# The first mixing of a two-block network: x scaled by its norm factor ahead of the transposes, raw x transposed a second time

## The chip, the core and the metric

The kernel runs on one core of a Trainium2 chip. The metric is device time in microseconds (us) of one execution; three runs of the kernel before gave 2796.80, 2799.38 and 2799.76 us, median 2799.38 us. TensorE multiplies matrices, VectorE and ScalarE work on elements, GpSimd does a few element operations beside them, and SyncE issues most transfers. In the profile they are PE (with PEld for its weight loads), DVE, ACT, POOL and SP.

## The reference, cut to what matters

Two blocks in float32 over 512 tokens of 1024 features. The change lies in the first block's mixing:

```python
h = rms_norm(x, attn_norm_w[i])          # x * rsqrt(mean(x*x) + eps) * w
g_q, g_k, g_v, g_z, g_b, g_a, s_u, d_q, d_k, d_v = split_cols(h @ w_in[i], IN_SIZES)
qkv = silu(causal_dwconv(concat([g_q, g_k, g_v]), gdn_conv_w[i]))   # 4 taps along the tokens
o_gdn = gated_delta_chunked(l2norm(g_q), l2norm(g_k), g_v, beta, log_decay)
o_gdn = rms_norm(o_gdn, gdn_norm_w[i]) * silu(g_z)
o_s5 = rms_norm(s5_mixer(s_u, ...), s5_norm_w[i])
o_diff = diff_attention(d_q, d_k, d_v, lam)
x = x + concat([o_gdn, o_s5, o_diff]) @ w_out[i]
x = x + conv_glu_ffn(rms_norm(x, ffn_norm_w[i]), ...)
```

Then come two layers of feed-forward, second mixing and feed-forward, and a last norm. The factor rsqrt(mean + eps), one number per token, can be applied to x before the product or to the columns of the product after it; both give the same result.

## The kernel before

Activations lie with features on the 128 partitions and the 512 tokens along the free axis, eight tiles for 1024 features. Every product of two float32 operands is made of three matmuls: each operand is split into a high part (rounded) and a low part (the rest), and `product` (L329 on) sums low weight times high x, high weight times low x and high times high. One product of 128 outputs is thus 8 times 3 = 24 matmuls of 512 columns, into one of the two PSUM buffers of tag `pp`. Each weight unit is loaded (`wr`), rounded on ScalarE (`wh`) and its rest taken on VectorE (`wl`); `wh` and `wl` have two buffers.

`first_load` brings x in as four blocks of 128 tokens, token on the partition. TensorE transposes them into all eight PSUM banks, and from the banks ScalarE makes the high parts `xgh` (times the gain) and VectorE the low parts `xgl`, in halves of 256 tokens; both engines then copy the raw x to `xT`. Square sums on ScalarE, an inverse square root in 10 small VectorE operations (`rsqrt`) and a spread over the partitions through TensorE (`spread`, tile `rT`) give `self.r`, the norm factor in every partition. So the first products start without the norm factor, and every reader of one multiplies by it afterwards on VectorE: `su` (four), `ab` (one), `dq`, `dk`, `dv` (four each), `gpad` (twelve, the convolution's padded input) and the gate `zs` in tile `gcv` (four).

`weave` (L346 on) writes the work of parts that run side by side in one order, by due times that each part yields; a scheduler then sets the final order of each engine, which is fixed before the run. The first mixing has two stages. In the first, the s5 tables are computed on VectorE, then four rounds of s5 (`WB`, `w4j`, `KT`, `ca`, `can`, `rho`, `z`), the gates and four heads of differential attention run side by side, with the 17 products as filler for TensorE. In the second, the four heads of the gated delta rule (`gdn`) do the same with their 16 products and those of the output weights. GpSimd makes `W` and `w4t` of s5, three operations for each round.

Of the kernel before, what the change touches and what calls it, by code (L numbers as in the profile page):

```python
# [244 lines left out]
class Net:  # L245
# [461 lines left out]
    def first_load(self, sp):  # L707

        nc, gain = self.nc, self.col["attn_norm"]
        self.sel = self.const.tile([128, 4, 128], F32, name="sel")  # L710
        nc.gpsimd.memset(self.sel, 0.0)
        nc.gpsimd.dma_start(out=self.sel[0:8], in_=self.A["sel"])
        one = self.tmp.tile([128, 128], F32, name="one", tag="sq")
        nc.gpsimd.memset(one, 1.0)
        self.ones = self.const.tile([128, 128], F32R, name="ones")
        nc.gpsimd.tensor_copy(out=self.ones, in_=one)

        zero = self.tmp.tile([128, 128], F32, name="zero", tag="sq")
        nc.gpsimd.memset(zero, 0.0)
        self.hl = self.const.tile([128, 128], F32R, name="hl")  # L720
        nc.gpsimd.tensor_copy(out=self.hl, in_=zero)
        blocks = []
        for n in range(4):
            src = self.A["x"][n * 128:n * 128 + 128]
            if n < 2:
                t = [self.op.tile([128, S], F32R, name=f"x{c}", tag=f"g{c}").bitcast(F32) for c in "hl"]
                for i in range(2):
                    nc.sync.dma_start(out=t[i], in_=src[:, i * S:i * S + S])
            else:
                w = self.wraw.tile([128, D], F32, name="wr", tag="wr")  # L730
                nc.sync.dma_start(out=w, in_=src)
                t = [w[:, :S], w[:, S:]]
            blocks.append(t)
        ps = [self.pp.tile([128, S], F32, name="pp", tag="pp") for _ in range(2)]
        ps += [f() for f in (self.ps, self.ps, self.ps, self.po, self.po, self.po)]
        v2, v = self.c4("v2", (128, 4, 2)), self.c4("cv")
        self.xs = [tuple(self.xgp.tile([128, S], F32R, name=f"xg{c}{k}", tag=f"xg{c}{k}") for c in "hl")
                   for k in range(KD)]
        at = lambda half, k, n=0, w=256: ps[4 * half + k // 2][:, 256 * (k % 2) + 128 * n:][:, :w]
        cs = [slice(256 * half, 256 * half + 256) for half in range(2)]  # L740
        for half, c in enumerate(cs):
            for n in range(2):
                for k in range(KD):
                    b = blocks[2 * half + n][k // 4]
                    nc.tensor.transpose(at(half, k, n, 128), b[:, (k % 4) * 128:(k % 4) * 128 + 128], self.ident)
            for k in range(KD):
                (h, l), g = self.xs[k], gain[:, k:k + 1]
                self.act(h[:, c], at(half, k), AF.Copy, scale=g)
                self.stt(l[:, c], at(half, k), g, h[:, c].bitcast(F32), ALU.mult, ALU.subtract)
        self.ready[12] = self.weights(self.A["w_in"][12], KD)  # L750
        for half, c in enumerate(cs):
            for k in range(KD):
                if k % 2:
                    nc.scalar.copy(out=self.xT[k][:, c], in_=at(half, k))
                else:
                    nc.vector.tensor_copy(out=self.xT[k][:, c], in_=at(half, k))
        for n in range(4):
            for i in range(2):
                sq = self.tmp.tile([128, S], F32, name="acc", tag="acc")
                self.act(sq, blocks[n][i], AF.Square, accum_out=v2[:, n, i:i + 1])  # L760
        self.tt(v, v2[:, :, 0], v2[:, :, 1], ALU.add)
        self.ts(v, v, 1.0 / D, ALU.mult, EPS, ALU.add)
        p = self.ps()
        self.at_once(self.spread(p, self.rsqrt(v)))
        self.r = self.bc.tile([128, S], F32, name="rstd", tag="rstd")
        nc.scalar.copy(out=self.r, in_=p)

    def out_after(self, outs, keys, w, pace=0):

# [8 lines left out]
        self.added.add(w)  # L778

    def proj(self, unit):  # L780
        return self.product(self.A["w_in"][unit], self.xs, self.ready.pop(unit, None))

    def scaled(self, pool, p, tag, bufs=None):
        t = pool.tile([128, S], F32, name=tag, tag=tag, bufs=bufs)
# [15 lines left out]
    def diff(self, dp, small, lane, nlam, outs):  # L800
        nc = self.nc
        gain = small.tile([128, 1], F32, name="dgain", tag=f"dgain{lane}", bufs=1)
        self.ts(gain, self.col["diff_norm"], 1.0 - LAM_INIT, ALU.mult)
        for h in (lane, lane + 2):
            slot = lambda name, k: self.x_slot(name, 4 * lane + k)
            ts = []
            for c, name in enumerate(("dq", "dk", "dv")):
                ts.append(slot(name, c))
                self.tt(ts[-1], self.proj(3 * h + c), self.r, ALU.mult)
                yield 5.2, (0, 0, 1.0)[c]  # L810
            qT, kT, vT = ts
            pv = self.transposed([vT[:, n * 128:n * 128 + 128] for n in range(4)])
            vt = slot("dvt", 3).rearrange("p (n v) -> p n v", n=4)
            nc.scalar.copy(out=vt, in_=pv.rearrange("p (n v) -> p n v", n=4))
            yield 0.25, 0
            po = self.po()
            eps = small.tile([128, 4], F32, name="eps", tag="eps", bufs=2)
            for qb in range(4):
                n = (qb + 1) * 128
                es = []  # L820
                for c in range(2):
                    rows = slice(64 * c, 64 * c + 64)
                    p = self.ps()
# [130 lines left out]
    def s5(self, sp, sq, tables, outs):  # L954
        nc = self.nc
        M = ALU.mult
        K, th8, pre, pim, B1, B2, C1, C2 = tables
        uts, ys = [], []
        for i in range(4):
            uts.append(self.scaled(sp, self.proj(12 + i), f"su{i}"))  # L960
            yield 5.2, 0
        pool = nc.gpsimd
        for i in range(4):
# [57 lines left out]
            self.reduced(sq, ca, [128, 512], "ca")  # L1021
            sn, cs = self.sincos(sq, ca, [128, 512], "ca")
            rho = sq.tile([128, 512], F32, name="rho", tag="rho")
            nc.vector.tensor_copy(out=v8(rho), in_=th8[:, 1, G].unsqueeze(2).to_broadcast(shc))
            nc.vector.memset(v8(rho)[:, :, 0:1], 0.0)
            yield 0.5, 1.0

# [63 lines left out]
    def gates(self, gc):  # L1091
# [1 line left out]
        M = ALU.mult  # L1093
        p = self.proj(16)
        ab = self.tmp.tile([8, S], F32, name="ab", tag="sq")
        self.tt(ab, p[0:8], self.r[0:8], M)
        yield 5.2, 1.0
        pt = self.ps()
        for n in range(4):
# [45 lines left out]
    def gdn(self, gf, gp, K, h, locks, outs):  # L1145
# [9 lines left out]
        for c in range(3):  # L1155
            p = self.proj(17 + 4 * h + c)
            i = 4 * c + h
            taps = self.col["gdn_conv"][:, 4 * i:4 * i + 4]
            pad = gf.tile([128, S + 3], F32, name="gpad", tag="gpad")
            nc.gpsimd.memset(pad[:, 0:3], 0.0)  # L1160
            self.tt(pad[:, 3:], p, self.r, M)
            cv = gf.tile([128, S], F32, name="gcv", tag="gcv")
            self.act(cv, pad[:, 3:], AF.Copy, scale=taps[:, 3:4])
            for t in (2, 1, 0):
                self.stt(cv, pad[:, t:t + S], taps[:, t:t + 1], cv, M, ALU.add)
            o = gf.tile([128, S], F32, name=f"g{c}", tag=f"g{c}")
            self.act(o, cv, AF.Silu)
            qkv.append(o)
            yield 5.2, 0
# [142 lines left out]
        self.stages += 1  # L1312
        third.n += 1
        yield from self.take(parked)
        zs = self.scaled(gf, self.proj(17 + 4 * h + 3), "gcv")
        self.act(zs, zs, AF.Silu)
        yield 5.2, 0
        self.stt(ss, ss, 1.0 / 128, vq, M, ALU.add)
        rr = self.rsqrt(ss)
# [211 lines left out]
```

## Time and profile before

| | |
|---|---|
| median of three runs | 2799.38 us |
| the profiled execution | 2799.44 us, span 2797.7 us |
| PE busy | 2723.6 us, 97% of the span |
| DVE busy | 1602.2 us, 57% |
| ACT busy | 1047.8 us, 37% |
| POOL busy | 167.4 us, 6% |
| chain that ended last | PE 87%, DVE 8%, ACT 2%, issue 2% |

A matmul of 512 columns stands in the records with 0.39 us, while the next one starts 0.23 us after it, so PE's busy time is no measure of how full it is where short gaps occur: the sum overlaps the gaps. The chain of waits shows better which engine the end depends on. The first mixing takes about 510 of the 2798 us; the rest of the program has the same instructions in both kernels.

### The profile page before, as it was taken

Reading aid. Unit: us, or ns where it says so; the run is one execution under the profiler, and the core shown is the slowest. Engines: PE = TensorE matmul, PEld = TensorE weight load, DVE = VectorE, ACT = ScalarE, POOL = GpSimd, SP = SyncE. Lnnn points to the kernel's source line nnn. Section 1 sums busy time; section 2 is a strip of 40 time slices with the busy share of each in tenths; the row PEclk is TensorE's granted clock in tenths of the full one; section 3 lists DMA queues with packets and bytes.
Section 4 is the critical chain, followed back from the end, with each engine's and each line's share of the span. In section 5 each row is a group of like instructions: output and inputs, shape, how many; then the busy total and the mean of one; then the engine's idle time right before and its main releaser. Section 6 shows DMA issues by size and latency. Waiting matters only on the chain.

```text
span 2797.7 us, 33414 instructions
## 1 busy us (share of the span) xinstructions
PE 2723.6 (97%) x12880; PEld 2188.6 (78%) x12880; DVE 1602.2 (57%) x2949; ACT 1047.8 (37%) x1712; POOL 167.4 (6%) x188
## 2 busy tenths in 40 slices
PE   8989999999999999999999999999999999999997
PEld 6667887788887888876778888888888766788886
DVE  8887865874666433447675434444344666643443
ACT  4556533442344322333453223333233345432223
POOL 1100000100001000012010000000000300100001
PEclk9999999999999999999999999999999999999999
DMA  5003110323323233231122232332333311323322
GB/s 185 27 20 106 61 39 27 110 96 90 101 88 101 98 89 108 84 119 57 34 78 96 89 102 98 90 103 92 100 98 89 102 38 45 100 98 89 107 84 82
DMA packets 83521, 239.13 MB, mean 85 GB/s; under 512 B 9304, under 2 KB 20952, under 8 KB 83232
## 3 DMA queue, kind: packets, MB, share of 16 engines
q1 hardware_dynamic: 82368, 233.53, 26.7%
q8 instruction: 101, 1.65, 0.2%
q0 software_dynamic: 416, 2.03, 0.2%
q10 hardware_dynamic: 576, 1.42, 0.1%
q14 instruction: 60, 0.49, 0.1%
HBM read 232.75 MB, written 4.19 MB: 85 GB/s over the span
## 4 chain that ended last, share of the span: by engine, by line
PE 87%; DVE 8%; ACT 2%; issue 2%; POOL 0%; DMA 0%; ACTq 0%; DVEq 0%; POOLq 0%
PE pp L288 75%; PE ps L288 6%; PE ps L481 2%; PE po L288 2%; DVE wl L291 2%; ACT wh L301 1%; ACT xgh L301 0%; DVE cr L298 0%; DVE ct L298 0%; DVE pd L291 0%; DVE xT L291 0%; DVE ct L291 0%; ACT sq L301 0%; DVE z L291 0%; POOL acc L291 0%
## 5 line engine op out<-in xcount | busy, mean ns | idle before, releaser
L301 ACT ACTIVATE wh<-wr 128x1024 fp32r<-128x1024 f32 (+6 forms) x543 | 476.8, 879 | 1288.4 <-PE pp L288 873.5
L288 PE MATMUL pp<-xgh,wl 128*128 128x512 f32 x2264 | 894.6, 395 | 16.7 <-DVE wl L291 8.0
L288 PE MATMUL pp<-xgh,wh 128*128 128x512 f32 x2264 | 887.8, 392 | 0.0
L288 PE MATMUL pp<-xgl,wh 128*128 128x512 f32 x2264 | 886.9, 392 | 0.0
L291 DVE TENSOR_TENSOR wl<-wr,wh 128x1024 fp32r<-128x1024 f32 (+6 forms) x543 | 548.1, 1010 | 269.5 <-ACT wh L301 263.3
L288 PEld LDWEIGHTS pp<-xgh,wl 128*128 128x128 f32 x2264 | 427.1, 189 | 112.3 <-DVE wl L291 10.7
L288 PEld LDWEIGHTS pp<-xgl,wh 128*128 128x128 f32 x2264 | 427.2, 189 | 90.2 <-issue 3.6
L288 PEld LDWEIGHTS pp<-xgh,wh 128*128 128x128 f32 x2264 | 427.1, 189 | 89.1 <-issue 1.2
L288 PE MATMUL pp<-gsl,wh 128*128 128x512 f32 x880 | 343.1, 390 | 0.0
L288 PE MATMUL pp<-gsh,wl 128*128 128x512 f32 x880 | 342.4, 389 | 0.0
L288 PE MATMUL pp<-gsh,wh 128*128 128x512 f32 x880 | 342.4, 389 | 0.0
L291 DVE TENSOR_TENSOR tu<-pp,rstd 128x512 f32<-128x512 f32 x88 | 60.8, 691 | 257.1 <-PE pp L288 257.1
L288 PEld LDWEIGHTS pp<-gsh,wl 128*128 128x128 f32 x880 | 165.2, 188 | 34.5
L288 PEld LDWEIGHTS pp<-gsh,wh 128*128 128x128 f32 x880 | 165.2, 188 | 34.2
L288 PEld LDWEIGHTS pp<-gsl,wh 128*128 128x128 f32 x880 | 165.2, 188 | 33.9
L291 DVE TENSOR_TENSOR tg<-pp,rstd 128x512 f32<-128x512 f32 x88 | 60.9, 692 | 183.3 <-PE pp L288 179.7
L298 DVE SCALAR_TENSOR_TENSOR xT<-pp,xT 128x512 f32<-128x512 f32 x64 | 44.3, 692 | 127.3 <-PE pp L288 127.3
L301 ACT ACTIVATE gsh<-gg 128x512 fp32r<-128x512 f32 x110 | 69.6, 633 | 99.0 <-DVE gg L291 98.9
L291 DVE TENSOR_TENSOR xT<-pp,xT 128x512 f32<-128x512 f32 x88 | 60.5, 688 | 63.4 <-PE pp L288 63.3
L288 PE MATMUL pp<-oh,wl 128*128 128x512 f32 x212 | 90.1, 427 | 6.7 <-ACT sgl L301 2.8
L301 ACT ACTIVATE e<-e,mx 128x256 f32<-128x256 f32 (+3 forms) x128 | 71.4, 558 | 43.2 <-DVE mx L612 42.6
L291 DVE TENSOR_TENSOR gsl<-gg,gsh 128x512 fp32r<-128x512 f32 x110 | 75.6, 687 | 19.5 <-ACT gsh L301 19.5
(443 smaller groups left out, 2640.1 us busy)
## 6 DMA issues: line engine op xcount, KB each, us to landing
wr<-in_f_up_dram SPq DMA_DIRECT2D x220, 512.0 KB, 3.3
wr<-in_w_in_dram SPq DMA_DIRECT2D x63, 512.0 KB, 3.4
wr<-in_f_d_dram SPq DMA_DIRECT2D x80, 384.0 KB, 3.1
wr<-in_f_d_dram SPq DMA_DIRECT2D x80, 320.0 KB, 2.8
wr<-in_wo_ds_dram SPq DMA_DIRECT2D x8, 512.0 KB, 3.2
wr<-in_wo_fox_dram SPq DMA_DIRECT2D x16, 192.0 KB, 2.3
wr<-in_wo_mla_dram SPq DMA_DIRECT2D x16, 192.0 KB, 2.3
xd<-xT SPq DMA_DIRECT2D x8, 256.0 KB, 4.6
```

The lines of the kernel that those rows point to most:

```text
L288: self.nc.tensor.matmul(out, lhsT=lhsT, rhs=rhs, start=start, stop=stop)
L291: (eng or self.nc.vector).tensor_tensor(out=out, in0=a, in1=b, op=op)
L298: self.nc.vector.scalar_tensor_tensor(out=out, in0=a, scalar=s, in1=b, op0=op0, op1=op1)
L301: self.nc.scalar.activation(out=out, in_=a, func=func, **kw)
L481: self.nc.tensor.transpose(p[:, n * 128:n * 128 + rows], b, self.ident[:rows, :rows])
```

## The change

Blocks of x are squared and their norm factor is computed first, two blocks at a time. Each half block is multiplied by it (tiles `xn`, the left half on VectorE, the right half on ScalarE) and then transposed, so that `xgh` and `xgl` carry the norm. `self.r` and its spread go. Raw x is transposed again, 32 transposes of 128 by 128, through `ps`, and copied to `xT` in whole tiles. Readers of a product no longer multiply: `su`, `ab`, `dq`, `dk`, `dv` are ScalarE copies, `zs` is made by the Silu directly, and the convolution reads its four taps out of PSUM. The copy `rho` of each s5 round goes from VectorE to ScalarE.

```diff
+        for half, room in enumerate(((self.pp_tile, self.pp_tile, self.ps, self.ps),
+                                     (self.ps, self.po, self.po, self.po))):
...
+            for n in two:
+                for i in range(2):
+                    self.act(sq, blocks[n][i], AF.Square, accum_out=v2[:, n, i:i + 1])
...
+            self.ts(v, v, 1.0 / D, ALU.mult, EPS, ALU.add)
+            r = self.rsqrt(v)
...
+                    if i:
+                        self.act(t, blocks[n][i], AF.Copy, scale=r[:, n:n + 1])
+                    else:
+                        self.ts(t, blocks[n][i], r[:, n:n + 1], ALU.mult)
+                    for k in range(4):
+                        nc.tensor.transpose(at(4 * i + k, m, 128), t[:, k * 128:k * 128 + 128], self.ident)
             for k in range(KD):
...
-        self.ready[12] = self.weights(self.A["w_in"][12], KD)
...
+        for k in range(KD):
+            p = self.transposed([blocks[n][k // 4][:, (k % 4) * 128:(k % 4) * 128 + 128] for n in range(4)])
...
-        p = self.ps()
-        self.at_once(self.spread(p, self.rsqrt(v)))
-        self.r = self.bc.tile([128, S], F32, name="rstd", tag="rstd")
-        nc.scalar.copy(out=self.r, in_=p)
...
-                self.tt(ts[-1], self.proj(3 * h + c), self.r, ALU.mult)
+                nc.scalar.copy(out=ts[-1], in_=self.proj(3 * h + c))
...
-            uts.append(self.scaled(sp, self.proj(12 + i), f"su{i}"))
+            uts.append(self.copied(sp, self.proj(12 + i), f"su{i}"))
...
-            nc.vector.tensor_copy(out=v8(rho), in_=th8[:, 1, G].unsqueeze(2).to_broadcast(shc))
+            nc.scalar.copy(out=v8(rho), in_=th8[:, 1, G].unsqueeze(2).to_broadcast(shc))
...
-            self.tt(pad[:, 3:], p, self.r, M)
...
-            self.act(cv, pad[:, 3:], AF.Copy, scale=taps[:, 3:4])
+            self.act(cv, p, AF.Copy, scale=taps[:, 3:4])
             for t in (2, 1, 0):
-                self.stt(cv, pad[:, t:t + S], taps[:, t:t + 1], cv, M, ALU.add)
+                self.stt(cv[:, 3 - t:], p[:, :S - 3 + t], taps[:, t:t + 1], cv[:, 3 - t:], M, ALU.add)
...
-        zs = self.scaled(gf, self.proj(17 + 4 * h + 3), "gcv")
-        self.act(zs, zs, AF.Silu)
+        self.act(zs, self.proj(17 + 4 * h + 3), AF.Silu)
```

How the order moves is seen at two places. The first is the start of the program on ScalarE (`acc` is a square with its sum, `xgh` the high part of a transposed tile, `xn` a scaled half block, `wh` a rounded weight). Before:

```order
L301 ACTIVATE acc,v_146<-xh 128x512
L301 ACTIVATE xgh_148<-pp,cols 128x256
L301 ACTIVATE xgh_152<-pp,cols 128x256
L301 ACTIVATE xgh_156<-ps,cols 128x256
L301 ACTIVATE xgh_150<-pp,cols 128x256
L301 ACTIVATE xgh_160<-ps,cols 128x256
```

And in the changed kernel, from the last two of its eight squares:

```order
L301 ACTIVATE acc,v_142<-xh 128x512
L301 ACTIVATE acc,v_142<-xl 128x512
L301 ACTIVATE xn_194<-xl,cr 128x512
L301 ACTIVATE xn_206<-xl,cr 128x512
L301 ACTIVATE wh<-wr 128x1024
L301 ACTIVATE lam<-lam 128x2
L301 ACTIVATE ea<-cols 128x4
L301 ACTIVATE xn_263<-xl,cr 128x512
L301 ACTIVATE xgh_143<-pp,cols 128x256
```

All eight squares, three of the four scalings and a weight's rounding now stand ahead of the first `xgh`, which had one square ahead of it.

The second place is the first s5 round on VectorE, from the end of `WB` to `KT`, whose readers on TensorE wait for it. Before:

```order
L291 TENSOR_TENSOR WB<-WB,w4t 128x1024
L291 TENSOR_TENSOR ca<-th_384,cst_s 128x512
L1024 COPY rho<-th_384 128x512
L295 TENSOR_SCALAR can<-ca 128x512
L1025 MEMSET rho 128x8
L291 TENSOR_TENSOR dv_848<-pp,rstd 128x512
L295 TENSOR_SCALAR can<-can 128x512
L291 TENSOR_TENSOR KT<-ps,cst_s 128x512
```

And in the changed kernel:

```order
L291 TENSOR_TENSOR WB<-WB,w4t 128x1024
L291 TENSOR_TENSOR ca<-th_439,cst_s 128x512
L1035 MEMSET rho 128x8
L295 TENSOR_SCALAR can<-ca 128x512
L295 TENSOR_SCALAR can<-can 128x512
L298 SCALAR_TENSOR_TENSOR ca<-can,ca 128x512
L291 TENSOR_TENSOR wl<-wr,wh 128x1024
L291 TENSOR_TENSOR KT<-ps,cst_s 128x512 x2
```

The copy to `rho` and the product's scaling `dv` are gone from between them; a weight's `wl` and one `ca` have come in ahead of `KT`. On TensorE 197 matmuls of products stood ahead of this round's first matmul before, and 172 stand there now.

## Rows read from the trace of the kernel before

**Rows 1.** Windows by stage: length, PE, PEld, DVE, ACT, POOL busy, clock, DMA
```profile
15.00:60.00 45.00, 43.19 (x179) 34.87 (x180) 42.76 (x123) 17.65 (x36) 2.13 (x1) 0.94 0.51 176
60.00:250.00 190.00, 170.03 (x1001) 127.55 (x1000) 155.55 (x347) 101.77 (x179) 30.26 (x17) 0.97 0.13 42
250.00:340.00 90.00, 89.07 (x499) 74.36 (x498) 79.55 (x200) 49.81 (x86) 2.01 (x13) 1.00 0.24 77
```

**Rows 2.** The chain's shares by line, 60 to 250 us, then 250 to 510
```profile
by line: PE pp L288 18.7%; PE ps L288 15.2%; PE po L288 12.0%; PE ps L481 4.6%; issue 4.2%; DVE wl L291 3.6%; DVE z L291 3.5%; DVE can L295 2.5%; DVE rho L1024 2.5%; DVE z L1039 2.4%; PE ps L1005 2.4%; DVE WB L291 1.9%; DVE e L612 1.7%; POO
...
by line: PE pp L288 50.4%; PE ps L288 31.1%; PE ps L481 5.9%; DVE gcv L298 1.6%; issue 1.5%; DVE xT L291 1.0%; PE ps L425 0.8%; DVE wl L291 0.8%; ACT sq L301 0.8%; DVE xgl L298 0.7%; PE po L288 0.6%; ACT xgh L301 0.6%; POOL acc L291 0.5%; P
```

**Rows 3.** Timeline of the first 20 us: start, length, instruction, [idle before it]
```profile
8.73 0.69 PE L745 MATMUL ps<-cst_i,wr 128*128 128x128 f32 x2 [0.33 <-DMA wr<-in_x_dram]
...
10.42 0.65 ACT L301 ACTIVATE acc<-xh 128x512 f32<-128x512 f32 x1
...
11.03 0.86 ACT L301 ACTIVATE xgh<-ps,cols 128x256 fp32r<-128x256 f32 x2
11.74 0.87 ACT L301 ACTIVATE xgh<-po,cols 128x256 fp32r<-128x256 f32 x2
12.46 1.11 ACT L301 ACTIVATE wh<-wr 128x1024 fp32r<-128x1024 f32 x1
13.40 0.53 ACT L301 ACTIVATE xgh<-ps,cols 128x256 fp32r<-128x256 f32 x1
...
15.34 0.80 PE L288 MATMUL pp<-xgh,wl 128*128 128x512 f32 x1 [4.14 <-ACT xT L754]
...
18.91 0.17 DVE L884 COPY dt<-s 128x32 f32<-128x32 f32 x1
```

**Rows 4.** Pieces of the chain: start, length, what; one product, eight transposes
```profile
257.48 5.47 PE pp L288 x24
...
318.41 0.87 PE ps L481 x8
```

**Rows 5.** Groups by line and shape: count, busy us, mean ns, idle before
```profile
L291 DVE TENSOR_TENSOR su<-pp,rstd 128x512 f32<-128x512 f32 x4 | 2.8, 689 | 0.1
...
L291 DVE TENSOR_TENSOR gpad<-pp,rstd 128x512 f32<-128x512 f32 x12 | 8.3, 689 | 4.4 <-PE pp L288 4.3
...
L298 DVE SCALAR_TENSOR_TENSOR gcv<-gpad,cols,gcv 128x512 f32<-128x512 f32 x36 | 26.5, 746 | 1.1 <-ACT gcv L301 1.1
...
L298 DVE SCALAR_TENSOR_TENSOR xT<-pp,xT 128x512 f32<-128x512 f32 x64 | 44.3, 692 | 127.3 <-PE pp L288 127.3
...
L1258 ACT COPY T<-ps 128x512 f32<-128x512 f32 x16 | 9.3, 583 | 12.2 <-PE ps L481 12.2
```

**Rows 6.** Instructions on tiles rho and cr: ns min/median/max, first and last start
```profile
L1024 DVE COPY rho<-th x4: 422/1334/2253, 65.4 to 172.2; 128x512 f32<-128x512 f32 x4
...
L291 DVE TENSOR_TENSOR ct<-cr x28: 152/161/167, 25.8 to 492.3; 128x4 f32<-128x4 f32 x28
```

**Rows 7.** Timeline around 65 and 175 us, GpSimd beside VectorE
```profile
64.92 2.41 POOL L291 TENSOR_TENSOR w4t<-pim,C 128x1024 f32<-128x1024 f32 x1 [4.57 <-DVE WB L291]
...
65.37 2.25 DVE L1024 COPY rho<-th 128x512 f32<-128x512 f32 x1
...
67.54 2.57 DVE L295 TENSOR_SCALAR can<-ca 128x512 f32<-128x512 f32 x1
...
174.94 1.95 DVE L298 SCALAR_TENSOR_TENSOR ct<-ct,cv 128x4 f32<-128x4 f32 x1
```

**Rows 8.** Waits of PE up to 520 us: total us, times, longest
```profile
PE ps L481 <- DVE KT L291: 3.6, 2, 3.2
...
PE ps L288 <- DVE rT L291: 1.3, 1, 1.3
```

**Rows 9.** Timeline of VectorE, one convolution: its scaling and its last tap
```profile
275.31 0.69 DVE L291 TENSOR_TENSOR gpad<-pp,rstd 128x512 f32<-128x512 f32 x1
...
289.28 0.74 DVE L298 SCALAR_TENSOR_TENSOR gcv<-gpad,cols,gcv 128x512 f32<-128x512 f32 x1
```

More of the change, by code (lines that the diff above doesn't have):

```diff
@@ L721, in first_load @@
         nc.gpsimd.tensor_copy(out=self.hl, in_=zero)
+        half_tile = lambda name, tag: self.op.tile([128, S], F32R, name=name, tag=tag).bitcast(F32)
         blocks = []
@@ L724, in first_load @@
             src = self.A["x"][n * 128:n * 128 + 128]
[L725 to L732, printed above, removed]
+            t = [half_tile(f"x{c}", f"g{c}") for c in "hl"]
@@ L733, in first_load @@
+            for i in range(2):
+                nc.sync.dma_start(out=t[i], in_=src[:, i * S:i * S + S])
             blocks.append(t)
-        ps = [self.pp.tile([128, S], F32, name="pp", tag="pp") for _ in range(2)]
-        ps += [f() for f in (self.ps, self.ps, self.ps, self.po, self.po, self.po)]
-        v2, v = self.c4("v2", (128, 4, 2)), self.c4("cv")
+        v2 = self.c4("v2", (128, 4, 2))
         self.xs = [tuple(self.xgp.tile([128, S], F32R, name=f"xg{c}{k}", tag=f"xg{c}{k}") for c in "hl")
@@ L738, in first_load @@
                    for k in range(KD)]
[L739 to L745, printed above, removed]
+        for half, room in enumerate(((self.pp_tile, self.pp_tile, self.ps, self.ps),
+                                     (self.ps, self.po, self.po, self.po))):
+            c = slice(256 * half, 256 * half + 256)
+            two = range(2 * half, 2 * half + 2)
+            for n in two:
+                for i in range(2):
+                    sq = self.tmp.tile([128, S], F32, name="acc", tag="acc")
+                    self.act(sq, blocks[n][i], AF.Square, accum_out=v2[:, n, i:i + 1])
+            v = self.c4("cv")
+            nc.vector.memset(v, 1.0)
+            self.tt(v[:, two[0]:two[0] + 2], v2[:, two[0]:two[0] + 2, 0], v2[:, two[0]:two[0] + 2, 1], ALU.add)
+            self.ts(v, v, 1.0 / D, ALU.mult, EPS, ALU.add)
+            r = self.rsqrt(v)
+            ps = [f() for f in room]
+            at = lambda k, n=0, w=256: ps[k // 2][:, 256 * (k % 2) + 128 * n:][:, :w]
+            for m, n in enumerate(two):
+                for i in range(2):
+                    t = half_tile(f"xn{i}", "o" + "hl"[i])
+                    if i:
[4 more added lines that the diff above has]
+                        nc.tensor.transpose(at(4 * i + k, m, 128), t[:, k * 128:k * 128 + 128], self.ident)
@@ L746, in first_load @@
             for k in range(KD):
                 (h, l), g = self.xs[k], gain[:, k:k + 1]
-                self.act(h[:, c], at(half, k), AF.Copy, scale=g)
-                self.stt(l[:, c], at(half, k), g, h[:, c].bitcast(F32), ALU.mult, ALU.subtract)
-        self.ready[12] = self.weights(self.A["w_in"][12], KD)
[L751 to L762, printed above, removed]
-        p = self.ps()
-        self.at_once(self.spread(p, self.rsqrt(v)))
-        self.r = self.bc.tile([128, S], F32, name="rstd", tag="rstd")
-        nc.scalar.copy(out=self.r, in_=p)
+                self.act(h[:, c], at(k), AF.Copy, scale=g)
@@ L768, in out_after, with pp_tile @@
+                self.stt(l[:, c], at(k), g, h[:, c].bitcast(F32), ALU.mult, ALU.subtract)
+        for k in range(KD):
+            p = self.transposed([blocks[n][k // 4][:, (k % 4) * 128:(k % 4) * 128 + 128] for n in range(4)])
+            if k % 2:
+                nc.scalar.copy(out=self.xT[k], in_=p)
+            else:
+                nc.vector.tensor_copy(out=self.xT[k], in_=p)
+    def pp_tile(self):
+        return self.pp.tile([128, S], F32, name="pp", tag="pp")
     def out_after(self, outs, keys, w, pace=0):
@@ L780, in proj, with copied @@
     def proj(self, unit):
-        return self.product(self.A["w_in"][unit], self.xs, self.ready.pop(unit, None))
+        return self.product(self.A["w_in"][unit], self.xs)
+    def copied(self, pool, p, tag):
+        t = pool.tile([128, S], F32, name=tag, tag=tag)
+        self.nc.scalar.copy(out=t, in_=p)
+        return t
     def scaled(self, pool, p, tag, bufs=None):
@@ L1095, in gates @@
         ab = self.tmp.tile([8, S], F32, name="ab", tag="sq")
-        self.tt(ab, p[0:8], self.r[0:8], M)
+        nc.scalar.copy(out=ab, in_=p[0:8])
         yield 5.2, 1.0
@@ L1158, in gdn @@
             taps = self.col["gdn_conv"][:, 4 * i:4 * i + 4]
-            pad = gf.tile([128, S + 3], F32, name="gpad", tag="gpad")
-            nc.gpsimd.memset(pad[:, 0:3], 0.0)
-            self.tt(pad[:, 3:], p, self.r, M)
             cv = gf.tile([128, S], F32, name="gcv", tag="gcv")
-            self.act(cv, pad[:, 3:], AF.Copy, scale=taps[:, 3:4])
+            self.act(cv, p, AF.Copy, scale=taps[:, 3:4])
             for t in (2, 1, 0):
-                self.stt(cv, pad[:, t:t + S], taps[:, t:t + 1], cv, M, ALU.add)
+                self.stt(cv[:, 3 - t:], p[:, :S - 3 + t], taps[:, t:t + 1], cv[:, 3 - t:], M, ALU.add)
             o = gf.tile([128, S], F32, name=f"g{c}", tag=f"g{c}")
@@ L1314, in gdn @@
         yield from self.take(parked)
-        zs = self.scaled(gf, self.proj(17 + 4 * h + 3), "gcv")
-        self.act(zs, zs, AF.Silu)
+        zs = gf.tile([128, S], F32, name="gzs", tag="gcv")
+        self.act(zs, self.proj(17 + 4 * h + 3), AF.Silu)
         yield 5.2, 0
```

## The prediction

> **What bounds the kernel now.** I read the windows by stage first, then the chain's shares, then the timeline of the front. Of the 190 us from 60 to 250 us PE's records leave 20 us idle and VectorE's 34 us; just before, from 15 to 60 us, VectorE is busy 42.76 of 45 us, and after it, from 250 to 340 us, PE 89.07 of 90 [rows 1]. PE's idle time is a floor, since a product of 24 matmuls takes 5.47 us, 0.228 us each [rows 4], while a record lasts longer. The chain tells the same with more contrast: from 60 to 250 us its listed PE lines add up to 53%, and wl, z, can, rho, the scan, WB and e on VectorE follow; from 250 to 510 us the PE lines are 89% [rows 2]. So in the s5 and attention stage TensorE and VectorE bound each other, and in the gated delta stage TensorE does nearly alone. The rest of the program is the same in both kernels and I give it nothing.
>
> **The front.** Before, the first product starts at 15.34 us [rows 3]. Now it needs the norm. Squares on ScalarE follow each other 0.61 us apart, a high part of 256 columns 0.36 us (two in 0.71), a weight's rounding 0.94 us, from start to start [rows 3]. The third block of x is there at 8.73 us [rows 3], so I put the end of the second block's last square at 7.9 us. Then come 12 dependent VectorE operations of 0.16 us [rows 6], 1.9 us, and the scaling of half blocks. No row shows that scaling on VectorE. The nearest are the unhindered copy from SBUF to SBUF, 0.42 us [rows 6], and a two-input operation of the same size, 0.69 us [rows 5]; I take 0.42, as it has one tensor input, and it is four times, so the upper end costs 1.1 us. On ScalarE I take 0.6 us, near the 0.583 us of a copy from PSUM [rows 5] and the 0.61 of a square.
>
> ScalarE then decides. It ends its eighth square at about 10.8 us and has before the first product is free to run: four scalings (2.4), 16 high parts (5.8), two weights (1.9), one xT copy (0.5) and small things (0.4), 11.0 us together, to 21.8 if never idle. The first product can start when most of that is done and is held between its first matmuls; I take an effective start of 21.0 us, 5.7 later. The bounds are 19 (3.7 later) if the two weights slip behind the high parts, and 24 if ScalarE is kept waiting once for each pair of blocks. VectorE's table work starts at 18.91 us before [rows 3]; it now stands behind the same low parts, the xT copies and one wl, and I take 25, 6 later.
>
> Of the 32 added transposes 16 stand on PE ahead of the first product's second matmul, in time in which it waits anyway; the other 16 stand between its matmuls, 16 times 0.109 us [rows 4], 1.75 us. The spread's transpose and matmul go (0.3 us), with the 1.3 us that PE waited for rT [rows 8]. **PE's line** is thus 5.7 + 1.75 - 0.3 - 1.3 = 5.8 us later when the stage is well under way.
>
> **VectorE's line.** It starts 6 us later and then has less to do up to the end of the stage: 17 products are no longer multiplied (4 su, 1 ab, 12 dq, dk and dv) at 0.69 us [rows 5], 11.7 us; the inverse square root (1.9) has moved into the front and the spread (0.7 for rT, 0.3 for the two small ones) is gone; one wl of 1.2 us is already done in the front. The four copies to rho are 0.42 to 2.25 us long [rows 6], 5.3 in all, and this is where I choose. The long one ran while GpSimd worked from 64.92 to 67.33 us and ended with it; the next operation, can, then took 2.57 us beside GpSimd's next one, and an operation on 4 columns took 1.95 us beside GpSimd too, where its like takes 0.16 [rows 6, 7]. The time over 0.42 us is GpSimd's, and what stands next on VectorE inherits it. I count 4 times 0.42, 1.7 us; the bounds are 1.7 and 5.3. VectorE's line is 6 - 11.7 - 1.9 - 1.0 - 1.2 - 1.7 = -11.5 us.
>
> The Trainium skill says the same of the cause (SBUF — State Buffer, Who interferes with whom): GpSimd and VectorE share one pair of SBUF ports, which an instruction holds for its whole length while the other is fully blocked; ScalarE has its own. It speaks against counting rho's whole 5.3 us, since can, which follows, is of the kind that it names. If the long copies were their own work, the line would be 3.6 us better.
>
> The added ScalarE copies (17 of 0.583 us and four to rho) are about 12 us beside 101.77 busy of 190 [rows 1, 5]; they follow the rounding of the next weight but one, which waits for the same product, so nothing waits longer there. If that cover is gone, one copy's wait is 0.6 us for what is behind it, exp above all.
>
> **The stage as a whole.** One line says +5.8, the other -11.5. As PE and VectorE are both near full and the order is woven from both, I take the middle, -2.9, rounded to -3. At the first KT this is seen: VectorE loses rho, dv and a stall there, where PE waited 3.6 us in all [rows 8], and PE comes with 25 matmuls (5.7 us) less done, which it owes later.
>
> **The gated delta stage.** VectorE loses 16 multiplications (12 gpad, 4 zs), 11.0 us; its taps read PSUM, where the same operation takes 0.692 us against 0.746 from SBUF [rows 5], 36 times, 1.9 us more. The Trainium skill (VectorE: DVE Perf Modes, Rules for kernel authors) advises copying a product to SBUF first where many operations read it; the trace has the PSUM form no slower, so by it the taps would cost more and by the rows they cost less. But VectorE is not what ends here: all lines other than PE's are 11% of the chain [rows 2]. Bounds 0 and -6; I take -2, near nothing, as the chain says.
>
> **Sum.** -3 - 2 = -5 us on the profiled execution's own 2799.44 us, which is 0.06 above the median: 2794.4 us.
>
> **Rivals.**
> 1. *VectorE's line decides.* For it: 42.76 of 45 us busy where the chain enters the stage. Against it: PE is idle for no longer than VectorE in the windows. Then -11.5 and -4: 2784 us.
> 2. *PE's line decides.* The late first product is never made up, because all holes that VectorE's relief opens are filled already. For it: PE 170 of 190 us. Then +5.8, nothing from the second stage, and up to 3 more if the first product starts at 24: 2805 to 2808.
> 3. *The taps hold the product's bank* (the slower side with a place of its own). In the convolution the bank was free after gpad, at 276.00 us; the last tap ended at 290.02, 14.7 us after the scaling began [rows 9]. Now the bank is held until the last tap. With two banks and 5.47 us a product, it decides from a hold of over 5.5 us: each such hold of 14 us costs up to 8.5. In the changed order the taps of the first three projections stand close behind each other, which speaks against it. Two such holds make +17, with the rest 2800 to 2811, mostly 2805.
> 4. *The relief is used up by the stalls.* GpSimd's twelve operations each stop one VectorE operation; if the one that is stopped is now on the chain of can and KT, rho's 1.7 us and two or three more are lost: 2798.
>
> **How the numbers follow.** Chances: forecast 0.45 (own range 2789 to 2800), rival 1 0.18, rival 2 0.17, rival 3 0.10, rival 4 0.10. A measurement of this kernel can tell about 0.2%, 5.6 us, from no change, so faster begins at 2793.8. The forecast lies at that edge and gives 0.25 to faster and 0.20 to no change; rival 1 is all faster; rival 4 gives 0.02 and 0.08; rivals 2 and 3 give 0.21 to slower and 0.06 to no change. Faster 0.45, same 0.34, slower 0.21. The range 2783 to 2809 leaves out the lower part of rival 1 and the upper part of 2 and 3.
>
> **What would show it.** In the profile after: the first product's start (21 us; after 24 rival 2 gains), the table work's start (25), the long VectorE operations beside GpSimd on can instead of rho, the first KT's matmuls about 2 us earlier than before, the time at which the last attention product ends, and PE's waits for a free pp bank behind gcv (over 5 us in all: rival 3). The forecast is wrong if the start of the second stage has moved by more than 8 us either way, or if that stage's length has changed by more than 6.

## The result and the profile after

The changed kernel takes 2821.86 us (median of four runs, 2820.20 to 2823.69) against 2799.35 us before: slower, ratio 1.0078, 95% interval 1.0066 to 1.0091, 22.5 us. The forecast was 2794.4 us with a range up to 2809, so neither its sign nor its range held. The profiled execution took 2820.20 us, its span is 2818.4 us.

The front came as forecast. Rows of the timeline after (start, length, engine, instruction), to be read beside [rows 3]:

```profile
3.70 0.63 ACT L301 ACTIVATE acc<-xh 128x512 f32<-128x512 f32 x1 [0.75 <-DMA xh<-in_x_dram]
...
10.62 1.32 ACT L301 ACTIVATE xn<-xl,cr 128x512 f32<-128x512 f32 x2
...
14.32 0.82 ACT L301 ACTIVATE xgh<-pp,cols 128x256 fp32r<-128x256 f32 x2
...
20.69 0.48 PE L288 MATMUL pp<-xgh,wl 128*128 128x512 f32 x1
...
26.21 0.17 DVE L894 COPY dt<-s 128x32 f32<-128x32 f32 x1
```

The first product starts at 20.69 us (forecast 21.0), the table work on VectorE at 26.21 (forecast 25). The windows by stage, with the columns of [rows 1], and one stretch of 10 us more:

```profile
15.00:60.00 45.00, 43.71 (x209) 36.02 (x210) 43.68 (x111) 21.66 (x39) 2.49 (x1) 1.00 0.40 143
60.00:250.00 190.00, 171.60 (x1003) 131.49 (x1002) 142.04 (x326) 107.40 (x191) 30.07 (x14) 0.96 0.14 44
250.00:340.00 90.00, 81.75 (x413) 65.70 (x411) 72.00 (x184) 44.76 (x80) 1.00 (x3) 0.94 0.23 76
290.00:300.00 10.00, 4.53 (x18) 3.70 (x18) 10.00 (x20) 3.61 (x4) 0.61 (x1) 0.68 0.03 4
```

Two things differ from [rows 1]. From 60 to 250 us VectorE is busy 142.04 us in place of 155.55, and TensorE is hardly busier for it. From 250 to 340 us TensorE falls from 89.07 to 81.75 of 90 us, and most of the loss lies between 290 and 300 us: 4.53 of 10 us, at a mean clock of 0.68 of full speed. The same stretch before:

```profile
290.00:300.00 10.00, 10.00 (x63) 8.51 (x62) 9.18 (x21) 3.26 (x8) 0.20 (x2) 1.00 0.12 42
```

To see where the 22.5 us arise I use two instructions that every kernel here has, and whose first and last starts a tile view gives: the scan `z`, once in each s5 round (its last is near the end of the first stage), and `goT`, whose last is the end of the last gated delta head. Before, then after (form, count, shortest, median and longest ns, first and last start):

```profile
L1039 DVE TENSOR_TENSOR_SCAN z<-rho,z x4: 1217/1220/1220, 95.9 to 195.5; 128x512 f32<-128x512 f32 x4
L298 DVE SCALAR_TENSOR_TENSOR goT<-ps,cols,gcv x8: 476/478/484, 394.9 to 496.0; 128x256 f32<-128x256 f32 x8
```

```profile
L1049 DVE TENSOR_TENSOR_SCAN z<-rho,z x4: 1216/1218/1224, 90.5 to 200.4; 128x512 f32<-128x512 f32 x4
L298 DVE SCALAR_TENSOR_TENSOR goT<-ps,cols,gzs x8: 473/476/483, 411.8 to 513.7; 128x256 f32<-128x256 f32 x8
```

The first scan is 5.4 us earlier than before, the last one 4.9 us later, the last `goT` 17.7 us later. So the first stage starts well and ends late, the delta stage loses 12.8 us, and a few more go at its end, where the first feed-forward starts. In the rest of the program nothing is lost: the lag is 22.8 us at the first `gsh` of the first feed-forward (533.2 and 556.0 us) and 21.4 at the last (2724.3 and 2745.7).

What happens at 290 us is seen on three engines (timeline after; the last bracket is idle time and what ended it):

```profile
280.20 0.39 PE L288 MATMUL pp<-xgh,wh 128*128 128x512 f32 x1
...
289.69 0.39 PE L288 MATMUL pp<-xgh,wh 128*128 128x512 f32 x1
292.17 1.01 PE L481 MATMUL ps<-cst_i,L 128*128 128x128 f32 x4 [2.10 <-DVE L L298]
296.56 1.97 PE L288 MATMUL ps<-X,L 128*128 128x64 f32 x8 [3.38 <-DVE X L291]
298.33 0.41 PE L450 MATMUL ps<-cst_i,hl 128*128 128x128 f32 x1
298.40 0.77 PE L288 MATMUL pp<-xgh,wl 128*128 128x512 f32 x1
...
288.91 0.68 ACT L301 ACTIVATE gcv<-pp,cols 128x512 f32<-128x512 f32 x1
...
293.92 0.73 DVE L298 SCALAR_TENSOR_TENSOR gcv<-pp,cols,gcv 128x511 f32<-128x511 f32 x1
294.57 0.68 DVE L291 TENSOR_TENSOR X<-ps,cst_m 128x512 f32<-128x512 f32 x1
295.17 0.73 DVE L298 SCALAR_TENSOR_TENSOR gcv<-pp,cols,gcv 128x510 f32<-128x510 f32 x1
295.83 0.68 DVE L291 TENSOR_TENSOR X<-cst_i,X 128x512 f32<-128x512 f32 x1
296.43 0.74 DVE L298 SCALAR_TENSOR_TENSOR gcv<-pp,cols,gcv 128x509 f32<-128x509 f32 x1
```

TensorE ends the sixth product of the delta stage at 290.1 us (the matmul that starts at 289.69 is its last) and waits twice for the first head's chain on VectorE. The next product starts at 298.40, after the last tap (296.43 + 0.74) has released the bank of the fifth, which had ended at 280.6 us and which the scaling began to read at 288.91. So this bank is held for 16.6 us, and from 290.1 to 297.2 us both product banks are held. The taps also stand between the steps of `X` that TensorE waits for. Before, this bank was read once and free at 276.00 us [rows 9], and a product filled the same two waits.

### The profile page after: what moved, and what is told of

It is laid out like the page before. It is cut to its first block, busy times and chain, and to the rows that moved or that the text cites. A ratio compares the mean times of both kernels' runs of the same rounds, so it can differ in the third digit from the quotient of the medians.

```text
span 2818.4 us, 33455 instructions
## 1 busy us (share of the span) xinstructions
PE 2731.9 (97%) x12910; PEld 2199.1 (78%) x12910; DVE 1586.4 (56%) x2923; ACT 1058.7 (38%) x1732; POOL 167.1 (6%) x176
## 4 chain that ended last, share of the span: by engine, by line
PE 85%; DVE 8%; ACT 3%; issue 2%; DMA 1%; POOL 0%; SPq 0%; ACTq 0%; DVEq 0%; POOLq 0%
PE pp L288 74%; PE ps L288 6%; PE ps L481 2%; PE po L288 2%; DVE wl L291 2%; ACT wh L301 1%; DVE cr L298 0%; ACT L301 0%; DVE xT L291 0%; DVE ct L298 0%; POOL W L291 0%; DVE ct L291 0%; DVE pd L291 0%; DVE z L291 0%; ACT xgh L301 0%
```

## The experiments

Theories. **A**: the delta masks `cst_m` come late. In the changed kernel their load stands behind the reloads of x on SP's queue and lands at 285 us, since the tiles `gpad` are gone and other tiles lie elsewhere in SBUF. **B**: taps that read PSUM hold the product's banks. **C**: the later front is never made up. **D**: ScalarE's new work (`rho`, `zs`, the copies) costs.

| run | us | ratio to before, interval |
|---|---|---|
| e1_masks_early | 2820.93 | 1.0078, 1.0065 to 1.0090 |
| e2_conv_sbuf | 2810.54 | 1.0039, 1.0025 to 1.0052 |
| e3_front_only | 2803.76 | 1.0014, 1.0005 to 1.0023 |
| e4_rho_vector | 2819.12 | 1.0068, 1.0055 to 1.0081 |
| e5_stage1_relief | 2805.44 | 1.0018, 1.0009 to 1.0026 |
| e6_three_banks | 2831.93 | 1.0108, 1.0094 to 1.0122 |
| e7_taps_first | 2819.92 | 1.0065, 1.0052 to 1.0078 |
| e8_before_rho | 2797.07 | 0.9989, 0.9980 to 0.9998 |
| e9_before_taps | 2810.82 | 1.0045, 1.0032 to 1.0057 |
| e10_conv_vector | 2809.84 | 1.0042, 1.0030 to 1.0055 |
| e11_mid_in_ps | 2818.55 | 1.0074, 1.0061 to 1.0088 |
| e12_before_relief | 2802.41 | 1.0013, 1.0004 to 1.0022 |
| e13_zs_scalar | 2810.21 | 1.0039, 1.0027 to 1.0052 |
| e14_front_no_raw | 2804.36 | 1.0023, 1.0014 to 1.0032 |

The kernel before, timed beside them, had medians from 2799.1 to 2799.8 us.

**e1, the masks.** To the changed kernel:

```diff
+                for _ in range(2):
+                    pad = gf.tile([128, S + 3], F32, name="gpad", tag="gpad")
+                    self.nc.gpsimd.memset(pad[:, 0:3], 0.0)
```

> The changed kernel, but the two unused padded conv tiles keep their room in SBUF. Every engine's order of compute stays as in the changed kernel; on SP's queue the load of the delta masks cst_m goes from behind the reloads of x (it landed at 282.2 us + 3.1) to row 17, ahead of the parking of x. Theory A (the masks come late, and the first head of the delta stage waits for them): VectorE's attn and L of the first head start some 3 us earlier, TensorE's two waits of 2.1 and 3.4 us for L and X go, the clock in 290:300 rises from 0.68 towards 1, and the time falls by 8 to 11 us to 2811-2814. Theory B (the conv taps, which hold the two pp banks, have pushed the products together, and the rest of the order on VectorE is serial): the masks take part in nothing, time within 3 us of 2821.9, and the two waits stay. Theory C (the later front): time within 3 us, lag at 230 us still +4.

No change, and the hole is still there:

```profile
290.00:300.00 10.00, 4.69 (x21) 3.54 (x20) 9.76 (x28) 3.85 (x6) 0.81 (x2) 0.77 0.00 0
```

Theory A falls. The chain of waits of the changed kernel names this load with 1.2% between 250 and 510 us, but VectorE waited only 0.16 us for it. In e1 the load is issued at 20.8 us, and TensorE's two waits there are still 1.9 and 3.4 us.

**e2, the taps from SBUF.** To the changed kernel:

```diff
+            pad = gf.tile([128, S + 3], F32, name="gpad", tag="gpad")
+            nc.gpsimd.memset(pad[:, 0:3], 0.0)
+            nc.scalar.copy(out=pad[:, 3:], in_=p)
-            self.act(cv, p, AF.Copy, scale=taps[:, 3:4])
+            self.act(cv, pad[:, 3:], AF.Copy, scale=taps[:, 3:4])
-                self.stt(cv[:, 3 - t:], p[:, :S - 3 + t], taps[:, t:t + 1], cv[:, 3 - t:], M, ALU.add)
+                self.stt(cv, pad[:, t:t + S], taps[:, t:t + 1], cv, M, ALU.add)
```

> The changed kernel, but ScalarE copies each projection to the padded tile in SBUF (12 more copies of about 0.58 us) and the taps read that, as before. The masks are loaded early too, as in the first run, so the difference to that run is the taps alone. Theory B: products stand between the delta steps again in TensorE's order; the lag against before falls from +15.9 at 283 us to +4 or less, time 2805-2812, at least 5 us below the first run. Theory A: same as the first run within 3 us (2811-2814). Theory C: lag of +4 at 230 us stays in any case.

2810.54, 11.3 us less than the changed kernel and 10.4 less than e1. B's time was met, although this adds twelve copies to ScalarE; its small lag was not, since the last `goT` still starts 9.6 us later than before (505.6).

**e9, the taps alone.** The same lines the other way round, in the kernel before.

> The kernel before, with one part of the change: the convolution's scaling and taps read the projection in PSUM, no padded tile. The norm factor is left out of the convolution (the rest keeps it), so the delta stage computes with unscaled q, k, v. Theory B (a product's bank is held from its end to the last tap, and while both banks are held no product fills TensorE's waits at the start of the delta stage): a lag of 10 to 16 us appears between 280 and 330 us and stays, time 2809-2817. Rival (the loss in the delta stage needs the changed first stage, whose end reaches it in another order): within 3 us of 2799.

2810.82, 11.7 us more than before. TensorE's waits from 240 to 340 us (total, times, longest) are those of the changed kernel, the wait for `X` with the same 3.4 us:

```profile
PE ps L288 <- DVE X L291: 3.4, 1, 3.4
PE ps L481 <- DVE L L298: 2.4, 1, 2.4
PE pp L288 <- DVE gcv L298: 1.9, 1, 1.9
```

```profile
280.00:290.00 10.00, 7.24 (x40) 5.59 (x38) 9.23 (x38) 6.73 (x17) 0.80 (x2) 1.00 0.32 113
290.00:300.00 10.00, 6.98 (x27) 6.00 (x28) 9.11 (x16) 2.55 (x3) 0.00 (x0) 0.66 0.16 52
```

The taps in PSUM thus cost 10 to 12 us by themselves, whichever first stage they follow.

**e6, e7, e11: three cures.** e6 changes `self.psum(es, 2, 6, 0)` to `self.psum(es, 3, 5, 0)`; e7 puts the scaling and taps under `with self.tc.high_priority(130):`; e11 gives the second projection of each head a bank of `ps`:

```diff
+            p = self.product(self.A["w_in"][17 + 4 * h + c], self.xs, p=self.ps() if c == 1 else None)
```

> The changed kernel, but in the delta stage the eight PSUM banks are split 3 for products and 5 for the rest in place of 2 and 6. Theory B (two banks held by taps leave no room for a product): lag at 283 us falls from +15.9 to +6 or less, the waits of TensorE of 2.1 and 3.4 us near 292-297 go or are filled by a product, time 2807-2813. Rival (the start of the delta work on VectorE, serial whatever the banks, decides): time 2818-2823. Second rival (five banks are too few for the delta steps): over 2823.

> The changed kernel, but ScalarE's scaling and the three taps of a projection get the priority that the weights' rounding has, so that they stand close behind the product on VectorE (a hold of about 0.6 + 3 x 0.7 = 2.7 us and the wait for VectorE, in place of 8 to 11 us). Theory B (the length of the hold decides): lag at 283-300 us down to +6 or less, time 2806-2813. Rival (the order of the delta steps on VectorE decides, the taps only fill it): 2818-2823; if taps that come first push the delta steps back, over 2823.

> The changed kernel, but the second of the three projections of each head is summed up in a bank of the other PSUM pool (six banks), so that the two pp banks carry two of three; the banks of the first stage stay as they are. Theory B: the hole of TensorE near 290-298 us gets a product, lag at 300 us +10 or less, time 2808-2815. If other things than banks keep the products away: 2818-2823. If the delta steps miss the bank: over 2823.

None gives the 11 us back. e7 shows the bank's wait most plainly:

```profile
291.22 0.40 PE L288 MATMUL pp<-xgh,wh 128*128 128x512 f32 x1
296.76 0.45 PE L481 MATMUL ps<-cst_i,L 128*128 128x128 f32 x1 [5.15 <-DVE L L298]
298.63 0.79 PE L288 MATMUL pp<-xgh,wl 128*128 128x512 f32 x1 [1.43 <-DVE gcv L298]
```

But e7 did not make the hold shorter, as it was meant to. The fifth product ends at 281.9 us, its scaling starts only at 294.5 on ScalarE, behind the head's own exp, and its last tap ends at 298.6, with taps of the sixth projection between its own. That is a hold of 16.7 us in place of 16.6, so e7 says nothing about a shorter one. e6 has the time of its second rival but not its mechanism. It loses earlier, near the change of stages, where the new split moves the projections back (the first scaling starts at 289.4 us in place of 249.9) and TensorE has 5.63 of 10 us left:

```profile
240.00:250.00 10.00, 5.63 (x22) 4.10 (x23) 7.59 (x24) 6.59 (x16) 0.00 (x0) 0.67 0.39 130
```

In e11 the stretch from 290 to 300 us is full again and a hole of the same size stands ahead of it (5.08 us busy from 280 to 290), where TensorE waits 4.57 us for a weight's `wl`. Each edit gave another fixed order with a hole of its own. That moving the taps to PSUM costs 10 to 12 us is shown by doing and undoing it (e2, e9). That it costs them through the held banks is read from the traces, in the wait for `gcv` and in the time at which the next product starts. No run made the hold shorter with the taps still in PSUM, and that one more bank is enough is not shown.

**e3, the front alone.** To the changed kernel: all evictions are VectorE copies, the convolution goes through `gpad`, rho is on VectorE.

```diff
-                nc.scalar.copy(out=ts[-1], in_=self.proj(3 * h + c))
+                nc.vector.tensor_copy(out=ts[-1], in_=self.proj(3 * h + c))
```

> Only the new front: blocks scaled ahead of the transposes, x transposed a second time; every eviction is on VectorE as a copy where before it was a product with the norm factor, the conv goes through the padded tile as before, rho is on VectorE. Theory C (the front's later first product and the second transposes give the lag of +4 at 190-230 us): lag +4 at 230 us, time 2802-2806. Rival (the lag at 230 us comes from ScalarE's new copies ahead of its other work, and the front is made good by 100 us): lag 0 to +1 at 230 us, time 2798-2801.

2803.76, 4.6 us more than before, theory C's number. Its lag is there at the end of the first stage and stays:

```profile
L1049 DVE TENSOR_TENSOR_SCAN z<-rho,z x4: 1217/1219/1224, 98.0 to 201.3; 128x512 f32<-128x512 f32 x4
L298 DVE SCALAR_TENSOR_TENSOR goT<-ps,cols,gzs x8: 475/477/484, 399.9 to 501.0; 128x256 f32<-128x256 f32 x8
```

**e14, without the second transposes.** To e3: `xT` is copied from the transposes of the scaled blocks.

> The run with the front alone (2803.8), without the second transposes: xT is copied from the transposes of the scaled blocks, so the residual starts from the normalized x in place of x. TensorE has 32 transposes less (16 of them stood between the first product's matmuls, 1.75 us by the rate of before). If the late first product costs the front's 4.6 us: 2802-2804. If the transposes and their copies do: 2799-2801.

2804.36, no gain within the intervals. But this run does not price the transposes alone. The copies to `xT` now stand ahead of a block's scaling on VectorE, TensorE waits 3.05 us for that block until 20.7 us, its granted clock falls to 0.50, and the first product starts at 21.94 us in place of e3's 20.60, its first nine matmuls 0.43 us apart or more. From 20 to 25 us, e3, then e14:

```profile
20.00:25.00 5.00, 4.70 (x32) 3.74 (x32) 4.78 (x10) 3.40 (x9) 0.00 (x0) 1.00 0.74 263
```

```profile
20.00:25.00 5.00, 4.18 (x11) 2.94 (x12) 4.30 (x12) 3.15 (x9) 0.00 (x0) 0.50 0.00 0
```

In e3, with transposes in that time, TensorE keeps its full clock, and the first product's last matmul starts even earlier (28.72 us against 29.34). So the late first product is in both runs, and whether my 1.75 us for the transposes were right is not shown.

**e5 and e12, the relief of VectorE.** e5 is e3 with the first stage's 17 evictions on ScalarE, as in the changed kernel; e12 has these in the kernel before:

```diff
-                self.tt(ts[-1], self.proj(3 * h + c), self.r, ALU.mult)
+                nc.scalar.copy(out=ts[-1], in_=self.proj(3 * h + c))
```

> New front, with the evictions of the first stage (su, ab, dq, dk, dv) on ScalarE as in the changed kernel; rho on VectorE as before; in the delta stage the projection is copied on VectorE to the padded tile and the taps read that, and zs is copied on VectorE, all as in the run with the front alone. Theory: the relief of VectorE in the first stage is real and worth 3 to 4 us, and all the rest of the loss sits in the delta stage: lag against before +1 to +2.5 at 230 us and the same at 520 us, time 2799-2802. Rival (relief worth nothing, the front's lateness stays): lag +5 at 230 us, time 2803-2805. Rival (the relief reorders the delta stage too): lag at 230 us small, at 520 us over +5, time over 2804.

> The kernel before, with its own front, and one part of the change: the 17 evictions of the first stage (su, ab, dq, dk, dv) are ScalarE copies. The norm factor is left out of these 17 tiles. Prediction's working (VectorE and TensorE bound the stage together, VectorE's line 11.7 us shorter, half of it gained): about 2793.5. Rival (TensorE's line and its own holes decide the first stage, VectorE's freed time turns into idle time, as the run of 2805.4 against that of 2803.8 suggests): 2798-2801, VectorE some 10 us less busy from 60 to 250 us. Second rival (ScalarE's copies stand ahead of exps, and TensorE's clock falls after the longer waits): 2801-2806.

e5 takes 2805.44, e12 2802.41, 3.2 us more than before. My theory (3 to 4 us gained) failed, and so did the prediction's number for e12. From 60 to 250 us e12 reads:

```profile
60.00:250.00 190.00, 172.68 (x1001) 132.03 (x1001) 141.73 (x333) 106.08 (x188) 30.94 (x16) 0.94 0.13 43
```

VectorE is 13.8 us less busy than in [rows 1], and TensorE has run the same number of matmuls, at a clock of 0.94 in place of 0.97. The scan tells how it went:

```profile
L1040 DVE TENSOR_TENSOR_SCAN z<-rho,z x4: 1215/1218/1226, 88.6 to 196.4; 128x512 f32<-128x512 f32 x4
```

The first round is 7.3 us earlier than before, the fourth 0.9 us later. The lead is mostly work put off: the first matmul that reads `KT` starts 4.1 us earlier (71.03 against 75.14 us), but 178 matmuls of products stand ahead of it in place of 198, and twenty at 0.228 us are 4.6 us. And the lower clock is not this one profile's: over the whole program it was 0.9906 on average in the 11 runs of e12 and 0.9924 in the 15 of the kernel before beside them. In all 75 runs of the kernel before, 0.001 of it goes with 2.1 us (a fitted line), so 0.0018 is about 3.7 us, an estimate that covers the 3.2 us lost. Why this order runs at a lower clock is not shown.

**e4, e8, e10, e13: ScalarE's other work.** e4 puts rho back on VectorE in the changed kernel, e8 puts it on ScalarE in the kernel before. e10 is e2 with the copy to `gpad` on VectorE. e13 is e5 with the gate as in the changed kernel:

```diff
-        nc.vector.tensor_copy(out=zs, in_=self.proj(17 + 4 * h + 3))
-        self.act(zs, zs, AF.Silu)
+        self.act(zs, self.proj(17 + 4 * h + 3), AF.Silu)
```

> The changed kernel, but rho is copied on VectorE, as before. The prediction's view (VectorE's line still counts in the first stage: 3 copies of 2.2 us beside GpSimd): the first stage is 2 to 6 us longer, time 2823-2828. Rival (VectorE has idle time there now, and rho on ScalarE delays its evictions): time 2816-2821, lag at 230 us down from +4 to +1. If rho decides nothing: 2822 within 2 us.

> The kernel before with one part of the change, rho copied on ScalarE. Prediction's view (four copies of 0.4 to 2.25 us leave VectorE, at least 1.7 us of its line): 2795-2798. Rival (ScalarE's copy of 512 columns stands ahead of evictions and exps that TensorE waits for; rho put back on VectorE gave 2.7 us in the changed kernel): 2800-2803. Neither: 2799 within 1.5.

> The changed kernel, but VectorE copies each projection to the padded tile and the taps read that; rho and zs stay on ScalarE. Beside the run that did this copy on ScalarE (2810.5) only the copy's engine differs; beside the run of 2805.4 only rho and zs. If ScalarE's copy is what costs (it stands in ScalarE's queue behind the exps of the delta steps and so holds the bank): 2804-2807. If rho and zs on ScalarE cost: 2809-2812.

> The kernel of the run at 2805.4 (new front, first stage's evictions on ScalarE, rho and the padded tile's copy on VectorE), with zs taken from PSUM by ScalarE's silu as in the changed kernel. If zs on ScalarE costs the 4.4 us up to 2809.8: 2808-2811. If rho on ScalarE costs them: 2804-2807. If each has a part: 2807-2808.

e4 (2819.12) lies in its rival's range. e10 (2809.84) is within the interval of e2: the copy's engine matters little. e13 (2810.21) lies 4.8 us over e5, and with rho on ScalarE as well (e10) there is no more: the gate taken from PSUM by ScalarE costs it, not rho. In the profiles the two have their last `goT` at about the same time (506.4 in e5, 506.1 in e13) and part at the start of the first feed-forward. e5, then e13:

```profile
520.00:540.00 20.00, 17.13 (x74) 13.10 (x75) 15.99 (x30) 9.65 (x13) 5.97 (x4) 1.00 0.35 117
```

```profile
520.00:540.00 20.00, 16.92 (x68) 12.15 (x67) 17.20 (x28) 7.53 (x12) 7.48 (x5) 0.93 0.48 154
```

How the Silu's read leads there I have not shown. e8 gains 2.7 us, as the prediction's view had it, and its interval just excludes no change; it is the one version faster than both kernels. In the changed kernel e4's 2.7 us the other way lie within the two intervals.

## Why the prediction was wrong

By medians, part after part, each a run less the one before it: new front +4.6 (e3), first stage's relief +1.7 (e5, within the intervals), the gate from PSUM +4.8 (e13), rho -0.4 (e10), ScalarE as the engine of the copy to `gpad` +0.7 (e2), taps from PSUM +11.3. They add up to the whole, 22.7, by the way they are taken (the kernel before had 2799.2 beside e3), so the sum confirms nothing.

- **Front and PE's line: right in size.** I put 5.8 us on PE's line; the front alone cost 4.6. One term was missing. Before, TensorE stood idle for 4.14 us ahead of the first product [rows 3] and ran the first ten of its matmuls at half its clock (0.50 from 15 to 20 us), about 0.43 us apart; after, the clock is 1.00 from 15 to 60 us in place of 0.94. That gave back some 2 us (ten times 0.2, an estimate), which I had not counted; with it the sum is 3.8, as near to 4.6 as 5.8 is.
- **VectorE's line: right in size, wrong in worth.** I put it 11.5 us shorter; of its terms 11.7 and 1.7 lie between 60 and 250 us, where VectorE was 13.5 us less busy. The first scan came 5.4 us earlier and the first matmul that reads `KT` 1.5 (73.68 us against 75.14; I had put 2).
- **"I take the middle": the step that failed first.** Nothing of VectorE's relief reached the end of the stage: e5 is no faster than e3, and e12 is 3.2 us slower than the kernel before. I let the time taken off VectorE count half without asking whether the operations taken off were on the chain. [rows 2] lists `wl`, `z`, `can`, `rho`, the scan, `WB` and `e`, and none of the 17 multiplications; in the whole chain from 60 to 250 us only one of them has more than 0.05 us:

```profile
230.87 0.70 DVE dv L291
```

Without them the order put the first s5 round ahead of products that TensorE then owed (e12). Rival 2 was the right one here; its 2805 to 2808 has e5's 2805.4 at its edge.
- **rho: right.** I counted 0.42 us a copy and left the rest to GpSimd. After, the long operations beside GpSimd are `can`, with 2.14 and 2.47 us for an operation whose median is 0.42. It is of a kind that the Trainium skill names as one that can want the ports shared with GpSimd (SBUF — State Buffer, Who interferes with whom), and the trace agrees:

```profile
64.16 2.42 POOL L291 TENSOR_TENSOR w4t<-pim,C 128x1024 f32<-128x1024 f32 x1 [4.56 <-DVE WB L291]
...
64.72 2.14 DVE L295 TENSOR_SCALAR can<-ca 128x512 f32<-128x512 f32 x1
...
66.89 2.47 DVE L295 TENSOR_SCALAR can<-can 128x512 f32<-128x512 f32 x1
```

- **The delta stage, "near nothing, as the chain says": the step that cost most.** The stage lost 12.8 us where I took -2, more than the 6 that I had named as a sign of being wrong. The chain showed that VectorE didn't end there; it could not show that this rested on two PSUM banks being freed at once. Rival 3 names this mechanism, with 17 us for two holds, and I gave it 0.10 since the first three projections' taps stand close together in the order. The costly hold was the fifth projection's, which I had in hand in [rows 9]: 16.6 us, half of them ahead of ScalarE's scaling. Its sign was misjudged as well: I named over 5 us of waits behind `gcv`, and the changed kernel and e9 have 1.9 each. The order is fixed with the hold already in it, so the product that is missing shows as waits for `L` and `X`. And a second part came from the first stage: from the last scan to the last `goT` the profiles have 299.7 to 301.6 us with the first stage's evictions on VectorE and the taps from SBUF (before, e3, e8, e14), and 303.7 to 305.1 with those evictions on ScalarE (e2, e5, e10, e12, e13). So the relief made a stage some 4 us longer whose instructions it does not touch; I gave that nothing, and why it does so is not shown.
- **The taps' own cost.** A tap from PSUM took 0.741 us (median of 36) against 0.746 from SBUF [rows 5], not 0.692: no gain there. The Trainium skill's advice (VectorE: DVE Perf Modes, Rules for kernel authors), to copy a product to SBUF first where many operations read it, turned out right here, for the bank and not for speed.
- **The gate.** I counted its VectorE time as gained and looked at no wait behind it; it cost 4.8 us (e13), by a way that stays open.
- **Rivals as exclusive cases.** PE's line (+5.8) and the holds (+17) concern two stages and could both come true. On 2799.4 they make 2822.2; 2821.9 was measured. That they meet so closely is luck, since the parts were 4.6 for the front, 11.3 for the taps, and 4.8 for the gate, which neither rival had. My cases joined rival 3 only with the forecast's gain, so this sum had no place in the range.

## What to carry to other kernels

Before counting time taken off an engine, look on the chain, by name, for the operations that are taken off; where they are not on it, as here, the time may buy nothing, however full the engine is. Before saving a copy out of PSUM, add the bank's hold, from the product's end to its last reader, and ask which product should run in that time. Rivals that concern different stages add up; give their sum a place in the range. When a cure brings nothing, look in the trace whether it did what it was for before taking the theory for refuted.

## What the runs showed of the hardware

Idle time of TensorE costs twice. The changed kernel waits from 290.1 to 292.2 us and from 293.2 to 296.6; its clock from 290 to 300 us is 0.68 on average, between its levels of 1.2 GHz (0.5) and 2.4 GHz, and the next product's matmuls of 512 columns start 0.43 us apart (298.97, 299.40, 299.82, 300.25) in place of 0.228. The front shows the same from 20 to 25 us: 1.00 in e3, which has transposes in the gap ahead of the first product, and 0.50 in e14, which idles there for 3.05 us.

And the clock differs between executions of one order. e4 and e5 have the same instructions in the same order up to the convolutions on PE, VectorE and ScalarE, and yet their last scans start at 197.8 and 202.5 us:

```profile
L1049 DVE TENSOR_TENSOR_SCAN z<-rho,z x4: 1217/1218/1226, 91.1 to 197.8; 128x512 f32<-128x512 f32 x4
```

```profile
L1049 DVE TENSOR_TENSOR_SCAN z<-rho,z x4: 1218/1220/1226, 91.7 to 202.5; 128x512 f32<-128x512 f32 x4
```

From 180 to 190 us alone, PE busy throughout in both, the clock was 1.00 in e4 and 0.75 in e5:

```profile
180.00:190.00 10.00, 9.99 (x60) 7.74 (x59) 6.74 (x14) 6.96 (x12) 0.00 (x0) 1.00 0.09 26
```

```profile
180.00:190.00 10.00, 10.00 (x48) 8.46 (x46) 8.11 (x16) 3.64 (x6) 0.00 (x0) 0.75 0.10 26
```

So lags read from a single profile of the first stage are good to some 5 us, and the shares above rest on medians. Why the clock fell in one and not in the other is open.
